# A linear attention kernel on one core: Q read in longer runs, norms and transposes moved, and another order in the last groups

## The chip, the cores and the metric

The kernel runs on one core of a Trainium2 chip. The time is the device time of one execution in microseconds (us). Each kernel was run several times, and a median is quoted with its range. The profile is of one of these executions; its span is about 1.8 us shorter than the time of that execution. A run is called slow when it lies more than 1.5% above the fastest of the same kernel. With one core there is no second die to compare with. Medians and ranges here are of all runs, slow ones too; ratios are of the fast runs alone.

The names of the engines in the profile: PE is TensorE, PEld its weight loads, DVE is VectorE, ACT is ScalarE, POOL is GpSimd, SP is SyncE.

## The reference

For each of 8 x 12 heads, with 512 rows of 64 numbers in Q, K and V:

```python
Q_feat = np.maximum(0, Q) + 1
K_feat = np.maximum(0, K) + 1
KV = np.einsum('bhkd,bhkv->bhdv', K_feat, V)
K_sum = np.sum(K_feat, axis=2)
numerator = np.einsum('bhqd,bhdv->bhqv', Q_feat, KV)
denominator = np.einsum('bhqd,bhd->bhq', Q_feat, K_sum)
return (numerator / (denominator[:, :, :, None] + 1e-10)).astype(np.float32)
```

All data are fp32 in HBM: 37.75 MB are read and 12.58 MB written.

## The kernel before

The 96 heads are worked in 12 groups of 8 heads. A group's work has these steps, each a function:

```python
def k_features(g):   # DVE: kf = max(K + 1, 1), two instructions
def v_blocks(g):     # V into a block layout: three copies on DVE, the fourth on ACT
def q_features(g):   # DVE: qf = max(Q + 1, 1), two instructions
def keys_values(g):  # PE: 32 matmuls into kva_ps, then four ACT copies into kva_diag
def transposes(g):   # PE: 16 transposes of qf into PSUM; ACT copies both halves to qt
def output(g):       # PE: 32 matmuls qt x kva_diag; DVE: 4 x (reciprocal, multiply) -> o_sb
```

K, V and Q are loaded for two groups at a time (the first and the last pair one group at a time), cast to bf16 on the way, from two buffers per tensor. A load is issued on POOL's queue as soon as its buffer is free. The instructions stand on each engine in the order of the program:

```python
for g in range(NG - 1):
    k_features(g)
    v_blocks(g)
    q_features(g)
    if g:
        transposes(g - 1)
    if g >= 2:
        output(g - 2)
    keys_values(g)
    if g % 2 and g // 2 + 2 < NG // 2:
        load_pair(g // 2 + 2)
    if g >= LAG:
        store(g - LAG)
last = NG - 1
k_features(last)
v_blocks(last)
transposes(last - 1)
output(last - 2)
q_features(last)
keys_values(last)
transposes(last)
output(last - 1)
output(last)
for g in range(last - LAG, NG):   # groups 10 and 11 in two halves each, from SP
    store(g)
```

In this text "the norms" are the reciprocal-multiply pairs of output, "K11" are the K features of group 11, "V10" is the copying of V of group 10 (with "lands", its transfer), and "group 10's matmuls" are the 32 of keys_values.

Of the kernel before, what the change touches and what calls it, by code (L numbers as in the profile page):

```python
# [9 lines left out]
BF16 = mybir.dt.bfloat16  # L10
# [9 lines left out]
def kernel(  # L20
# [15 lines left out]



    nc = tc.nc

    B, H, S, D = Q.shape
    P = 128
    C = 8
    C2 = 2 * C
    NPAIR = B * H * S // (P * C)
    NP = 4
    NG = NPAIR // NP
    D1 = D + 1
    W = 2 * D1

    def view(t, c):
        return t.flatten_outer_dims().rearrange("(n p c) d -> p n c d", p=P, c=c)

    q_dram = view(Q, C2)
    k_dram = view(K, C2)
    v_dram = view(V, C2)
    o_dram = view(out, C)
# [1 line left out]
    const = ctx.enter_context(tc.tile_pool(name="const", bufs=1))  # L59
    head_pool = ctx.enter_context(tc.tile_pool(name="head_pool", bufs=1))  # L60
    in_pool = ctx.enter_context(tc.tile_pool(name="in_pool", bufs=IN_BUFS))
    feat_pool = ctx.enter_context(tc.tile_pool(name="feat", bufs=2))
    mid_pool = ctx.enter_context(tc.tile_pool(name="mid", bufs=3))
    out_pool = ctx.enter_context(tc.tile_pool(name="out_pool", bufs=OUT_BUFS))
    recip_pool = ctx.enter_context(tc.tile_pool(name="recip", bufs=4))
    psum_kva = ctx.enter_context(tc.tile_pool(name="psum_kva", bufs=2, space=bass.MemoryType.PSUM))
# [1 line left out]
    psum_qt = ctx.enter_context(tc.tile_pool(name="psum_qt", bufs=2, space=bass.MemoryType.PSUM))  # L68

    identity = const.tile([P, P], BF16, name="identity")  # L70
    NV = 3
    v_all = const.tile([P, 9, 2, C2, D], BF16, name="v_all")
    v_blk = [v_all[:, 5 * i : 5 * i + 4] for i in range(2)]
    ones = const.tile([P, 4], BF16, name="ones")
    zero = const.tile([P, 1], FP32, name="zero")
    kva_diag = [const.tile([P, 4, 2, D1], BF16, name=f"kva_diag{i}") for i in range(NV)]

    drams = dict(k=k_dram, v=v_dram, q=q_dram)
    raw = {}
    kfs = {}  # L80
    qfs = {}
    qts = {}
    outs = {}

    def own(g):
        return slice(g % 2 * 2, g % 2 * 2 + 2)

    def load_first_k():
        k_raw = head_pool.tile([P, 2, C2, D], FP32, name="k_first")
        nc.sync.dma_start(out=k_raw, in_=k_dram[:, 0:2])  # L90
        raw["k", 0] = k_raw

    def load(s, groups, names="kvq"):
        ms = slice(groups[0] % 2 * 2, groups[-1] % 2 * 2 + 2)
        for x in names:
            if (x, "buf", s) not in raw:
                raw[x, "buf", s] = in_pool.tile([P, 4, C2, D], BF16, name=f"{x}_raw")
            t = raw[x, "buf", s]
            nc.gpsimd.dma_start(  # L99
                out=t[:, ms], in_=drams[x][:, 2 * groups[0] : 2 * groups[-1] + 2]  # L100
            )
            for g in groups:
                raw[x, g] = t[:, own(g)]

    def load_pair(s):
        if s < NG // 2 - 1:
            load(s, (2 * s, 2 * s + 1))
        else:
            load(s, (2 * s,))
            load(s, (2 * s + 1,))  # L110

    def store(g):
        o_sb = outs.pop(g)
        o_to = o_dram[:, g * NP : g * NP + NP]
        if g < NG - 2:
            nc.gpsimd.dma_start(out=o_to, in_=o_sb)  # L116
            return
        for h in range(2):
            nc.sync.dma_start(out=o_to[:, h:NP:2], in_=o_sb[:, h:NP:2])

    def feature(dst, src):
        nc.vector.tensor_scalar(  # L122
            out=dst, in0=src, scalar1=1.0, scalar2=1.0, op0=ALU.add, op1=ALU.max
        )

    def k_features(g):
        k_raw = raw.pop(("k", g))
        kf = feat_pool.tile([P, C2, 2, D], BF16, name="kf")
        for n in range(2):
            feature(kf[:, :, n], k_raw[:, n])  # L130
        kfs[g] = kf

    def v_blocks(g):
        v_raw = raw.pop(("v", g))
        for b in range(4):
            ps = slice(32 * b, 32 * b + 32)
            if b == 3:
                nc.scalar.copy(out=v_blk[g % 2][ps, b], in_=v_raw[ps])  # L138
            else:
                nc.vector.tensor_copy(out=v_blk[g % 2][ps, b], in_=v_raw[ps])  # L140

    def q_features(g):
        q_raw = raw.pop(("q", g))
        qf = feat_pool.tile([P, C2, 2, D], BF16, name="qf")
        for half in range(2):
            cs = slice(half * C, half * C + C)
            feature(qf[:, cs].rearrange("p c n d -> p n c d"), q_raw[:, :, cs])
        qfs[g] = qf

    def keys_values(g):  # L150
        kf = kfs.pop(g)
        sb = g % 2
        vb = v_all[:, 4 * sb : 4 * sb + 5]
        kva_ps = psum_kva.tile([P, 5, D], FP32, name="kva_ps")
        for c in range(C2):
            for n in range(2):
                nc.tensor.matmul(  # L157
                    kva_ps[64 * n : 64 * n + 64],
                    lhsT=kf[:, c, n, :],
                    rhs=vb[:, :, n, c, :],  # L160
                    start=(c == 0),
                    stop=(c == C2 - 1),
                )
        kva = kva_diag[g % NV]
        for n in range(2):
            ps = slice(64 * n, 64 * n + 64)
            nc.scalar.copy(out=kva[ps, :, n, 0:D], in_=kva_ps[ps, sb : sb + 4, :])  # L167
            nc.scalar.copy(out=kva[ps, :, n, D], in_=kva_ps[ps, 4 - 4 * sb, 0:4])  # L168

    def transposes(g):  # L170
        qf = qfs.pop(g)
        qt = mid_pool.tile([P, C, P, 2], BF16, name="qt")
        for half in range(2):
            qt_ps = psum_qt.tile([P, C, P], BF16, name="qt_ps")
            for c in range(C):
                nc.tensor.transpose(qt_ps[:, c, :], qf[:, half * C + c, :, :], identity)  # L176
            nc.scalar.copy(out=qt[:, :, :, half], in_=qt_ps)  # L177
        qts[g] = qt

    def output(g):  # L180
        kva = kva_diag[g % NV]
        qt = qts.pop(g)
        o_sb = out_pool.tile([P, NP, C, D], FP32, name="o_sb")
        for h in range(2):
            ops = [psum.tile([P, 2, BANK], FP32, tag="ps", name="o_ps") for _ in range(2)]
            for c in range(C):
                for j in range(2):
                    b = 2 * h + j
                    nc.tensor.matmul(  # L189
                        ops[c // 4][64 * j : 64 * j + 64, c // 2 % 2, (c % 2) * W : (c % 2) * W + W],  # L190
                        lhsT=qt[:, c, 32 * b : 32 * b + 32, :],
                        rhs=kva[:, b],
                        start=True,
                        stop=True,
                    )
            for i in range(2):
                cells = ops[i][:, :, 0 : 2 * W].rearrange("p b (c n x) -> p b c n x", n=2, x=D1)
                recip = recip_pool.tile([P, 2, 2, 2, 1], FP32, name="recip")
                nc.vector.reciprocal(out=recip, in_=cells[:, :, :, :, D:D1])  # L199
                nc.vector.tensor_tensor(  # L200
                    out=o_sb[:, h:NP:2, 4 * i : 4 * i + 4].rearrange(
                        "p n (b c) d -> p b c n d", b=2
                    ),
                    in0=cells[:, :, :, :, 0:D],
                    in1=recip.to_broadcast([P, 2, 2, 2, D]),
                    op=ALU.mult,
                )
        outs[g] = o_sb
# [9 lines left out]
    with tc.manual_schedule():  # L218
        nc.gpsimd.memset(zero, 0.0)
        load_first_k()  # L220
        load(0, (0,), "vq")
        load(0, (1,))
        nc.vector.memset(ones, 0.0)
        for b in range(4):
            nc.vector.memset(ones[32 * b : 32 * b + 32, b : b + 1], 1.0)  # L225
        clear(0, 3, 5)
        e = v_all[:, 4, :, :, 0:4].rearrange("p n c j -> p (n c) j")
        nc.vector.tensor_copy(out=e, in_=ones[:, None, :].to_broadcast([P, 2 * C2, 4]))
        make_identity(nc, identity)
        for t in kva_diag:  # L230
            nc.gpsimd.memset(t, 0.0)  # L231
        load_pair(1)
        clear(5, 7, 9)
        for g in range(NG - 1):
            k_features(g)
            v_blocks(g)
            q_features(g)
            if g:
                transposes(g - 1)
            if g >= 2:  # L240
                output(g - 2)
            keys_values(g)
            if g % 2 and g // 2 + 2 < NG // 2:
                load_pair(g // 2 + 2)
            if g >= LAG:
                store(g - LAG)
        last = NG - 1
        k_features(last)
        v_blocks(last)
        transposes(last - 1)  # L250
        output(last - 2)
        q_features(last)
        keys_values(last)
        transposes(last)
        output(last - 1)
        output(last)
        for g in range(last - LAG, NG):
            store(g)
# [30 lines left out]
```

## Time and profile before

| what | before |
|---|---|
| time, median of 4 runs | 127.41 us (127.02 to 128.06) |
| span of the profiled run | 125.8 us |
| DVE busy | 88.2 us (70%) |
| ACT busy | 68.0 us (54%) |
| PE busy | 65.2 us (52%) |
| mean rate of the HBM over the span | 400 GB/s |
| last DVE instruction ends | 120.36 us |
| last store lands | 124.87 us |

DVE is the busiest engine that computes, and yet it is idle for nearly a third of the span. The list of DVE's waits (who waited for whom: us in total, times, longest) says why:

```profile
DVE v_all L140 <- DMA v_raw<-in_V_dram: 10.6, 3, 5.3
DVE qf L122 <- DMA q_raw<-in_Q_dram: 6.5, 4, 2.9
...
DVE recip L199 <- PE o_ps L189: 4.8, 4, 1.7
```

It waits for loads, and only 4.8 us for PE. The prediction shows the other lines.

### The profile page before, as it was taken

The numbers are of one execution on the slowest core, as the hardware profiler recorded it, in microseconds if no ns is written. First come the engines' busy times: TensorE is split into PE (matmuls) and PEld (weight loads), VectorE is DVE, ScalarE is ACT, GpSimd is POOL, SyncE is SP. The second block draws the span as 40 slices with busy tenths as digits, with TensorE's granted clock in tenths as the row PEclk, the third lists the DMA queues.
The fourth block names the chain that finished last, engine by engine and source line by source line (L and its number), as shares of the span: only waits on it lengthen the run. The fifth ranks groups of instructions, "written<-read, shape, count | busy, mean of one in ns | idle before, by whom it ended". The sixth has DMA issues, their size and how long they took to land.

```text
span 125.8 us, 2337 instructions
## 1 busy us (share of the span) xinstructions
PE 65.2 (52%) x960; PEld 48.4 (39%) x960; DVE 88.2 (70%) x188; ACT 68.0 (54%) x87; POOL 27.8 (22%) x43
## 2 busy tenths in 40 slices
PE   0005939000059784796918476006978569694500
PEld 0003627000036564574806365004656447472300
DVE  4896280206199799999989990629959999758920
ACT  7832296006700889629892962750087971987000
POOL 6990213000002082023700260212221002020000
PEclk9999999755555999689999999955589976999955
DMA  3999999999999999999999999999999999999991
GB/s 76 341 211 209 210 213 211 210 212 211 212 211 212 211 214 212 210 212 214 253 414 287 209 210 212 213 369 380 209 210 210 211 287 418 418 417 410 403 391 72
DMA packets 13419, 32.13 MB, mean 255 GB/s; under 512 B 608, under 2 KB 608, under 8 KB 13408
## 3 DMA queue, kind: packets, MB, share of 16 engines
q0 software_dynamic: 12048, 28.84, 98.3%
q1 hardware_dynamic: 1360, 3.15, 6.8%
q8 instruction: 7, 0.11, 0.3%
q14 instruction: 4, 0.03, 0.1%
HBM read 37.75 MB, written 12.58 MB: 400 GB/s over the span
## 4 chain that ended last, share of the span: by engine, by line
DMA 40%; DVE 26%; PE 18%; POOL 6%; issue 6%; DVEq 0%; POOLq 0%
DMA q_raw<-in_Q_dram 40%; DVE o_sb L200 15%; PE kva_ps L157 11%; DVE v_all L140 4%; PE qt_ps L176 3%; DVE recip L199 3%; PE o_ps L189 3%; POOL v_raw L99 2%; DVE qf L122 2%; DVE kf L122 2%; POOL q_raw L99 1%; POOL kva_diag L231 1%; POOL k_raw L99 1%; POOL identity masks.py:199 0%; POOL identity masks.py:197 0%
## 5 line engine op out<-in xcount | busy, mean ns | idle before, releaser
L157 PE MATMUL kva_ps<-v_all,kf 128*64 128x320 bf16 x384 | 36.4, 356 | 13.1 <-DVE v_all L140 13.1
L189 PE MATMUL o_ps<-kva_diag,qt 128*64 128x130 bf16 x384 | 19.1, 234 | 40.9 <-DVE o_sb L200 40.4
L200 DVE TENSOR_TENSOR o_sb<-o_ps,recip 128x512 f32<-128x512 f32 x48 | 33.2, 692 | 1.6
L140 DVE COPY v_all<-v_raw 32x2048 bf16<-32x2048 bf16 x36 | 26.5, 736 | 10.9 <-DMA v_raw<-in_V_dram 10.6
L157 PEld LDWEIGHTS <-kf 128*64 128x64 bf16 x384 | 25.3, 133 | 20.9 <-DVE v_all L140 13.3
L189 PEld LDWEIGHTS <-qt 128*64 128x64 bf16 x384 | 12.7, 114 | 46.4 <-DVE o_sb L200 44.6
L138 ACT COPY v_all<-v_raw 32x2048 bf16<-32x2048 bf16 x12 | 22.7, 1894 | 13.3 <-DMA v_raw<-in_V_dram 13.1
L177 ACT COPY qt<-qt_ps 128x1024 bf16<-128x1024 bf16 x24 | 29.7, 1308 | 0.3
L167 ACT CAST kva_diag<-kva_ps 64x256 bf16<-64x256 f32 x24 | 8.9, 371 | 33.3 <-PE kva_ps L157 33.2
L122 DVE TENSOR_SCALAR qf<-q_raw 128x1024 bf16<-128x1024 bf16 x24 | 9.1, 423 | 6.6 <-DMA q_raw<-in_Q_dram 6.5
L99 POOL DMA_DIRECT2D k_raw<-in_K_dram x7 | 5.3, 754 | 38.1 <-DVE kf L122 37.3
L116 POOL DMA_DIRECT2D out_dram<-o_sb x10 | 8.4, 846 | 22.6 <-DVE o_sb L200 16.4
L176 PE MATMUL qt_ps<-identity,qf 128*128 128x128 bf16 x192 | 13.1, 222 | 0.0
L199 DVE RECIPROCAL recip<-o_ps 128x8 f32<-128x8 f32 x48 | 9.6, 199 | 4.9 <-PE o_ps L189 4.8
L122 DVE TENSOR_SCALAR kf<-k_raw 128x1024 bf16<-128x1024 bf16 x22 | 8.7, 437 | 6.0 <-DMA k_raw<-in_K_dram 6.0
L176 PEld LDWEIGHTS <-qf 128*128 128x128 bf16 x192 | 11.0, 99 | 3.3 <-issue 3.0
L99 POOL DMA_DIRECT2D v_raw<-in_V_dram x8 | 6.1, 764 | 18.8 <-ACT v_all L138 10.7
L99 POOL DMA_DIRECT2D q_raw<-in_Q_dram x8 | 5.9, 741 | 4.2 <-DMA q_raw<-in_Q_dram 4.2
L213 DVE MEMSET v_all<- 128x3072 f32 (+1 forms) x2 | 4.4, 2192 | 1.1 <-DVE ones L225 0.7
L168 ACT CAST kva_diag<-kva_ps 64x4 bf16<-64x4 f32 x24 | 4.0, 169 | 0.0
L214 ACT COPY v_all<-zero 128x2048 f32<-128x2048 f32 x2 | 3.7, 1894 | 0.0
L214 ACT ACT_TABLE_LOAD x1 | 1.3, 1283 | 0.7 <-PEq L273 0.7
(12 smaller groups left out, 4.6 us busy)
## 6 DMA issues: line engine op xcount, KB each, us to landing
out_dram<-o_sb POOLq DMA_DIRECT2D x10, 1024.0 KB, 20.2
k_raw<-in_K_dram POOLq DMA_DIRECT2D x4, 1024.0 KB, 18.0
v_raw<-in_V_dram POOLq DMA_DIRECT2D x4, 1024.0 KB, 20.9
q_raw<-in_Q_dram POOLq DMA_DIRECT2D x4, 1024.0 KB, 25.0
v_raw<-in_V_dram POOLq DMA_DIRECT2D x4, 512.0 KB, 17.3
q_raw<-in_Q_dram POOLq DMA_DIRECT2D x4, 512.0 KB, 17.1
out_dram<-o_sb SPq DMA_DIRECT2D x4, 512.0 KB, 5.1
k_raw<-in_K_dram POOLq DMA_DIRECT2D x3, 512.0 KB, 23.3
```

Of the source, the lines that this page charges most:

```text
L99: nc.gpsimd.dma_start(out=t[:, ms], in_=drams[x][:, 2 * groups[0] : 2 * groups[-1] + 2])
L116: nc.gpsimd.dma_start(out=o_to, in_=o_sb)
L122: nc.vector.tensor_scalar(out=dst, in0=src, scalar1=1.0, scalar2=1.0, op0=ALU.add, op1=ALU.max)
L138: nc.scalar.copy(out=v_blk[g % 2][ps, b], in_=v_raw[ps])
L140: nc.vector.tensor_copy(out=v_blk[g % 2][ps, b], in_=v_raw[ps])
L157: nc.tensor.matmul(kva_ps[64 * n : 64 * n + 64], lhsT=kf[:, c, n, :], rhs=vb[:, :, n, c, :], start=(c == 0), stop=(c == C2 - 1),)
L167: nc.scalar.copy(out=kva[ps, :, n, 0:D], in_=kva_ps[ps, sb : sb + 4, :])
L176: nc.tensor.transpose(qt_ps[:, c, :], qf[:, half * C + c, :, :], identity)
L177: nc.scalar.copy(out=qt[:, :, :, half], in_=qt_ps)
L189: nc.tensor.matmul(ops[c // 4][64 * j : 64 * j + 64, c // 2 % 2, (c % 2) * W : (c % 2) * W + W], lhsT=qt[:, c, 32 * b : 32 * b + 32, :], r ...
L199: nc.vector.reciprocal(out=recip, in_=cells[:, :, :, :, D:D1])
L200: nc.vector.tensor_tensor(out=o_sb[:, h:NP:2, 4 * i : 4 * i + 4].rearrange("p n (b c) d -> p b c n d", b=2), in0=cells[:, :, :, :, 0:D], i ...
```

## The change

The intent: fewer and longer reads for Q, DVE work (the norms of group g-2) moved into the time in which DVE waits for V, and a tail with shorter waits. In full that is:

- Q of groups 2 to 9 is loaded with 8 KB runs in HBM. One run now holds rows of both groups of a pair, so the output of one group needs the kva_diag of both (four of them in place of three). The copies of the transposes now read PSUM with a stride and write qt in order, where they read in order and wrote every second element.
- For even groups output(g-2) stands ahead of V's copies. For odd groups transposes stand on both sides of the output, and both groups' Q features are taken at once.
- In the last pair K and V are loaded in one transfer for both groups. Group 10's V copies stand behind output 8, its Q features and transposes ahead of K11 and V11, and DVE copies the second half of the transposes of groups 10 and 11 where ACT did both halves.

```diff
+    q_eights = view(Q, C4)
...
+    def load_q(s):
+        t = in_pool.tile([P, 4, C2, D], BF16, name="q_raw").rearrange(
+            "p (n r) (q c) d -> p n (r q c) d", n=2, c=C
+        )
+        nc.gpsimd.dma_start(out=t, in_=q_eights[:, 2 * s : 2 * s + 2])
...
     def load_pair(s):
-        if s < NG // 2 - 1:
-            load(s, (2 * s, 2 * s + 1))
-        else:
-            load(s, (2 * s,))
-            load(s, (2 * s + 1,))
+        pair = (2 * s, 2 * s + 1)
+        load("k", pair)
+        load("v", pair)
+        if eights(2 * s):
+            load_q(s)
+        else:
+            for g in pair:
+                load("q", (g,))
...
+            copy = nc.vector.tensor_copy if half and g >= NG - 2 else nc.scalar.copy
+            copy(out=qts[g][:, lo : lo + CC // 2], in_=qt_ps.rearrange("p c r q -> p c q r"))
...
+        for g in range(last):
+            if g and not eights(g - 1):
+                transposes(g - 1)
+            elif eights(g) and g % 2:
+                transposes(g - 1)
             k_features(g)
-            v_blocks(g)
-            q_features(g)
-            if g:
-                transposes(g - 1)
+            if g % 2:
+                v_blocks(g)
+            if not eights(g) and g < last - 1:
+                q_features(g)
             if g >= 2:
                 output(g - 2)
+            if g % 2 == 0:
+                v_blocks(g)
+            elif eights(g):
+                transposes(g)
+            if eights(g) and g % 2 == 0:
+                q_features(g)
+                q_features(g + 1)
             keys_values(g)
...
+        q_features(last - 1)
+        transposes(last - 1)
         k_features(last)
         v_blocks(last)
-        transposes(last - 1)
         output(last - 2)
+        keys_values(last)
         q_features(last)
-        keys_values(last)
         transposes(last)
```

eights(g) is true for groups 2 to 9. Cuts are marked with "..."; declarations of pools, and how Q, qt and the stores are addressed, are left out.

More of the change, by code (lines that the diff above doesn't have):

```diff
@@ L44 @@
     C2 = 2 * C
+    C4 = 4 * C
     NPAIR = B * H * S // (P * C)
@@ L61 @@
     in_pool = ctx.enter_context(tc.tile_pool(name="in_pool", bufs=IN_BUFS))
-    feat_pool = ctx.enter_context(tc.tile_pool(name="feat", bufs=2))
-    mid_pool = ctx.enter_context(tc.tile_pool(name="mid", bufs=3))
+    kf_pool = ctx.enter_context(tc.tile_pool(name="kf_pool", bufs=2))
+    qf_pool = ctx.enter_context(tc.tile_pool(name="qf_pool", bufs=3))
+    mid_pool = ctx.enter_context(tc.tile_pool(name="mid", bufs=2))
     out_pool = ctx.enter_context(tc.tile_pool(name="out_pool", bufs=OUT_BUFS))
@@ L70 @@
     identity = const.tile([P, P], BF16, name="identity")
-    NV = 3
+    NV = 4
     v_all = const.tile([P, 9, 2, C2, D], BF16, name="v_all")
@@ L79 @@
     raw = {}
+    bufs = {}
     kfs = {}
@@ L83, with eights @@
     outs = {}
+    def eights(g):
+        return 2 <= g < NG - 2
     def own(g):
-        return slice(g % 2 * 2, g % 2 * 2 + 2)
+        return slice(g % 2, 4, 2) if eights(g) else slice(g % 2 * 2, g % 2 * 2 + 2)
     def load_first_k():
@@ L91, in load_first_k, with load @@
         raw["k", 0] = k_raw
-    def load(s, groups, names="kvq"):
+    def load(x, groups):
+        s = groups[0] // 2
+        if groups[0] % 2 == 0 or (x, s) not in bufs:
+            bufs[x, s] = in_pool.tile([P, 4, C2, D], BF16, name=f"{x}_raw")
         ms = slice(groups[0] % 2 * 2, groups[-1] % 2 * 2 + 2)
-        for x in names:
-            if (x, "buf", s) not in raw:
-                raw[x, "buf", s] = in_pool.tile([P, 4, C2, D], BF16, name=f"{x}_raw")
-            t = raw[x, "buf", s]
-            nc.gpsimd.dma_start(
-                out=t[:, ms], in_=drams[x][:, 2 * groups[0] : 2 * groups[-1] + 2]
-            )
-            for g in groups:
-                raw[x, g] = t[:, own(g)]
-    def load_pair(s):
-        if s < NG // 2 - 1:
-            load(s, (2 * s, 2 * s + 1))
-        else:
-            load(s, (2 * s,))
-            load(s, (2 * s + 1,))
+        nc.gpsimd.dma_start(
+            out=bufs[x, s][:, ms], in_=drams[x][:, 2 * groups[0] : 2 * groups[-1] + 2]
+        )
+        for g in groups:
+            raw[x, g] = bufs[x, s][:, own(g)]
+    def load_q(s):
+        t = in_pool.tile([P, 4, C2, D], BF16, name="q_raw").rearrange(
+            "p (n r) (q c) d -> p n (r q c) d", n=2, c=C
+        )
+        nc.gpsimd.dma_start(out=t, in_=q_eights[:, 2 * s : 2 * s + 2])
+        rows = t.rearrange("p n (r c) d -> p n r c d", c=C)
+        for e in range(2):
+            raw["q", 2 * s + e] = rows[:, :, :, 4 * e : 4 * e + 4]
+    def load_pair(s):
+        pair = (2 * s, 2 * s + 1)
[3 more added lines that the diff above has]
+            load_q(s)
+        else:
+            for g in pair:
+                load("q", (g,))
     def store(g):
         o_sb = outs.pop(g)
-        o_to = o_dram[:, g * NP : g * NP + NP]
+        first = 2 * NP * (g // 2)
+        o_to = o_dram[:, first + g % 2 : first + 2 * NP : 2] if eights(g) else o_dram[
+            :, g * NP : g * NP + NP
+        ]
         if g < NG - 2:
@@ L127, in k_features @@
         k_raw = raw.pop(("k", g))
-        kf = feat_pool.tile([P, C2, 2, D], BF16, name="kf")
+        kf = kf_pool.tile([P, C2, 2, D], BF16, name="kf")
         for n in range(2):
@@ L143, in q_features @@
         q_raw = raw.pop(("q", g))
-        qf = feat_pool.tile([P, C2, 2, D], BF16, name="qf")
-        for half in range(2):
-            cs = slice(half * C, half * C + C)
-            feature(qf[:, cs].rearrange("p c n d -> p n c d"), q_raw[:, :, cs])
+        if not eights(g):
+            q_raw = q_raw.rearrange("p n (r c) d -> p n r c d", c=C)
+        R, CC = q_raw.shape[2:4]
+        qf = qf_pool.tile([P, R, CC, 2, D], BF16, name="qf")
+        for n in range(2):
+            feature(qf[:, :, :, n], q_raw[:, n])
         qfs[g] = qf
@@ L171, in transposes @@
         qf = qfs.pop(g)
-        qt = mid_pool.tile([P, C, P, 2], BF16, name="qt")
-        for half in range(2):
-            qt_ps = psum_qt.tile([P, C, P], BF16, name="qt_ps")
-            for c in range(C):
-                nc.tensor.transpose(qt_ps[:, c, :], qf[:, half * C + c, :, :], identity)
-            nc.scalar.copy(out=qt[:, :, :, half], in_=qt_ps)
-        qts[g] = qt
+        R, CC = qf.shape[1:3]
+        if R == 4 and g % 2:
+            qts[g] = qts[g - 1]
+        else:
+            qts[g] = mid_pool.tile([P, C, P, R], BF16, name=f"qt{R}")
+        first = g % 2 * CC if R == 4 else 0
+        for half in range(2):
+            qt_ps = psum_qt.tile([P, CC // 2, R, P], BF16, name="qt_ps")
+            for c in range(CC // 2):
+                for r in range(R):
+                    nc.tensor.transpose(
+                        qt_ps[:, c, r], qf[:, r, half * CC // 2 + c, :, :], identity
+                    )
+            lo = first + half * CC // 2
+            copy = nc.vector.tensor_copy if half and g >= NG - 2 else nc.scalar.copy
+            copy(out=qts[g][:, lo : lo + CC // 2], in_=qt_ps.rearrange("p c r q -> p c q r"))
     def output(g):
-        kva = kva_diag[g % NV]
         qt = qts.pop(g)
@@ L187, in output @@
                 for j in range(2):
-                    b = 2 * h + j
+                    if eights(g):
+                        b = 2 * (g % 2) + j
+                        kva = kva_diag[(g // 2 * 2 + h) % NV]
+                        q = slice(16 * (4 * h + b), 16 * (4 * h + b) + 16)
+                    else:
+                        b = 2 * h + j
+                        kva = kva_diag[g % NV]
+                        q = slice(32 * b, 32 * b + 32)
                     nc.tensor.matmul(
                         ops[c // 4][64 * j : 64 * j + 64, c // 2 % 2, (c % 2) * W : (c % 2) * W + W],
-                        lhsT=qt[:, c, 32 * b : 32 * b + 32, :],
+                        lhsT=qt[:, c, q, :],
                         rhs=kva[:, b],
@@ L220 @@
         load_first_k()
-        load(0, (0,), "vq")
-        load(0, (1,))
+        load("v", (0,))
+        load("q", (0,))
+        for x in "kvq":
+            load(x, (1,))
         nc.vector.memset(ones, 0.0)
@@ L233 @@
         clear(5, 7, 9)
-        for g in range(NG - 1):
+        last = NG - 1
+        for g in range(last):
[3 more added lines that the diff above has]
+                transposes(g - 1)
             k_features(g)
-            v_blocks(g)
-            q_features(g)
-            if g:
-                transposes(g - 1)
+            if g % 2:
+                v_blocks(g)
+            if not eights(g) and g < last - 1:
+                q_features(g)
             if g >= 2:
                 output(g - 2)
+            if g % 2 == 0:
[5 more added lines that the diff above has]
+                q_features(g + 1)
             keys_values(g)
@@ L246 @@
                 store(g - LAG)
-        last = NG - 1
+        q_features(last - 1)
+        transposes(last - 1)
         k_features(last)
         v_blocks(last)
-        transposes(last - 1)
         output(last - 2)
+        keys_values(last)
         q_features(last)
-        keys_values(last)
         transposes(last)
```

## The prediction

> **What bounds the kernel now.** I read the page's slices first, then a table of stretches, then the chain of waits, then the groups.
>
> ```profile
> DMA  3999999999999999999999999999999999999991
> GB/s 76 341 211 209 210 213 211 210 212 211 212 211 212 211 214 212 210 212 214 253 414 287 209 210 212 213 369 380 209 210 210 211 287 418 418 417 410 403 391 72
> HBM read 37.75 MB, written 12.58 MB: 400 GB/s over the span
> ```
>
> The DMA engines are busy from the second slice to the last but one. A load counts by what it writes (bf16, half of what it reads), so 212 GB/s of loads is 424 GB/s of HBM reads; stores run at about 418. One group's share of one tensor is 1.05 MB on the HBM side, and one such unit takes 1.05 MB / 0.42 = 2.5 us of the DMA, load or store. There are 48 units: 48 x 2.5 = 120 us of a 125.8 us span. The rest is about 2 us before the first packet and the end.
>
> ```profile
> 102.00:104.00 2.00, 1.91 (x22) 1.42 (x24) 1.93 (x7) 0.95 (x1) 0.00 (x0) 0.58 1.07 350
> 104.00:106.00 2.00, 2.00 (x20) 1.42 (x18) 1.97 (x5) 0.00 (x0) 0.75 (x1) 0.56 1.03 420
> 116.00:118.00 2.00, 0.94 (x20) 0.64 (x22) 1.90 (x7) 0.00 (x0) 0.00 (x0) 1.00 1.02 413
> 120.00:122.00 2.00, 0.00 (x0) 0.00 (x0) 0.36 (x1) 0.00 (x0) 0.00 (x0) 0.50 1.00 387
> 122.00:124.00 2.00, 0.00 (x0) 0.00 (x0) 0.00 (x0) 0.00 (x0) 0.00 (x0) 0.50 0.60 234
> ```
>
> Columns: stretch, length, busy us (count) of PE, PEld, DVE, ACT, POOL, then granted clock, DMA share, GB/s. The last loads land near 104 us; after that there are only stores, back to back until about 123. Compute (DVE) stops at 120.36 and the DMA still works off what was queued.
>
> ```profile
> 59.53 24.54 DMA q_raw<-in_Q_dram
> ...
> 87.24 4.27 PE kva_ps L157 x32
> ...
> 102.55 3.81 PE kva_ps L157 x32
> ...
> 109.99 2.17 PE kva_ps L157 x32
> ...
> 119.67 0.69 DVE o_sb L200
> ```
>
> This is the chain that ended last: start, length, what. It is a chain of compute from 84.07 (Q of groups 8 and 9 lands: 59.53 + 24.54) to 120.36. But the completion events of the stores in the trace come every 2.5 us (1.27 us for the half-size ones) right up to the last at 124.87, so the chain is not late: the DMA would end there even if compute ended sooner. How much sooner or later? An unloaded half-size store takes, from this trace, 1.07 us (issue to first packet, at the head) + 1.27 + 0.32 (last packet to completion) = 2.7 us. 124.87 - 2.7 = 122.2: compute has about 1.8 us of slack and no more. The same 32 matmuls take 2.2 us at full clock and 3.8 to 4.3 when the clock column says about 0.5. That matters below.
>
> ```profile
> L200 DVE TENSOR_TENSOR o_sb<-o_ps,recip 128x512 f32<-128x512 f32 x48 | 33.2, 692 | 1.6
> L140 DVE COPY v_all<-v_raw 32x2048 bf16<-32x2048 bf16 x36 | 26.5, 736 | 10.9 <-DMA v_raw<-in_V_dram 10.6
> L177 ACT COPY qt<-qt_ps 128x1024 bf16<-128x1024 bf16 x24 | 29.7, 1308 | 0.3
> L122 DVE TENSOR_SCALAR kf<-k_raw 128x1024 bf16<-128x1024 bf16 x22 | 8.7, 437 | 6.0 <-DMA k_raw<-in_K_dram 6.0
> ```
>
> DVE's bill per group: K features 0.7, V copies 3 x 0.736 = 2.2, Q features 0.76, an output of four reciprocal-multiply pairs 4 x 0.84 = 3.4 (each pair starts 0.84 after the last).
>
> [...] stores in 4 KB packets run at 418 to 420 GB/s, those in 2 KB packets near 413. [...] its halved stretches last 3.41 us or multiples, and windows with less than about half PE work were followed by one. [...] No such bf16 copy on DVE is in this trace; 512 fp32 elements from PSUM took 0.692, so I estimate 1.15 us for 1024 elements.
>
> **The change part by part.**
>
> Q in 8 KB runs. 8 groups, 8 x 128 x 2 = 2048 reads of 4 KB become 1024 of 8 KB. Over 16 engines that is 64 packets fewer each[...]
>
> Order in the middle. DVE takes the output of g-2 before it waits for V and Q of an even group, and both Q features at once. That moves 3.4 us of DVE work into its idle stretches (from 75.7 to 84.1 before) and frees Q's buffers sooner. But the DMA queue holds at least 7 us of issued work at each load's issue, from the issue times and the rate. So nothing in the middle is on the path: zero.
>
> One more clearing on POOL (0.5 us at about 7 us) lies under the 15 us of loads already queued: zero.
>
> The tail. Three things change. First, the last pair's loads become K10+11, V10+11, Q10, Q11 instead of K10, V10, Q10, K11, V11, Q11. Second, DVE does output 8 before V10. Third, DVE takes half of the transposes' copies of groups 10 and 11, and in DVE's order the copy for group 10 stands ahead of K11 and V11, waiting for PE. I walk it with the durations above:
> - Q of 8 and 9 lands at 83.9. Two stores, K10+11 and V10+11 follow, 6 units. The trace's completion of the sixth unit is 99.7 (before, it was K11); less 0.2 is 99.5. Before, V10 was there at 94.8.
> - Q 8 and 9 features, K9, V9, output 7: DVE done near 92. It waits for K10+11 (94.6), does output 8 to about 99.8, then V10 to 102.0.
> - PE's 32 matmuls for group 10 start at 102.0, after about 4 us with almost no PE work, so at half clock: 4.2 us, to 106.2. Transposes 1.2: 107.4. DVE, idle since 102.9, copies: 108.5.
> - K11 0.7, V11 2.3: 111.5. Output 9: 114.9. PE, again idle for 4 us, starts group 11's matmuls behind output 9's last ones at 113.8: cold to 118.0. Transposes to 119.2, DVE copy to 120.3 (idle since its Q11 features at 115.7).
> - Outputs 10 and 11: 6.9 us, 127.2.
>
> Compute would end at 127.2 instead of 120.4. Of these 6.8 us, 1.8 go into the slack and 5.0 reach the end: span 127.2 + 2.7 + 0.9 (last completion to end of span, as before) = 130.8; plus 1.75 between span and time (127.54 - 125.8) makes 132.6.
>
> **The rivals.**
> 1. The clock stays up. With group 11's matmuls at full clock (2.4) compute ends at 125.4 and the time is 130.8; with both groups' so, 123.4 and 128.8. For it: 3.4 us windows fall by chance. Against it: group 10's start comes after two windows with well under half PE work, and the like was followed by half clock every time.
> 2. The DMA stays the bound to the end. [...] For it: the DMA was saturated through the whole of before, and the author tuned the tail. Against it: DVE's work after V10 lands, without any wait, is 2.2 + 0.76 + 1.15 + 0.7 + 2.3 + 3.4 + 0.76 + 1.15 + 6.9 = 19.3 us, so 118.9, and two waits for PE of at least 2 us each exceed the slack.
> 3. The 8 KB runs are worth far more than I can see, for instance 5% of Q's 20 us: 1 us, and all landings move up by as much: about 126.6 where the DMA binds, 131.6 where compute does. [...]
>
> **Range and chances.** Both cold 132.6 (one half), one warm 130.8 (a quarter), both warm 128.8 (a twentieth), DMA-bound 127.3 or near (a fifth): mean 130.9. Below 127.3 there is little room, above 133 only if the DVE copy is dearer than estimated. Over 2% slower begins at 130.1: 0.58; within 2%: 0.39; over 2% faster (125.0) would need 2.5 us less DMA time: 0.03.
>
> **What would show it.** Right: DMA saturated and GB/s as before until 104, then a hole in the last slices; output 8 ahead of V10; DVE idle before the group 10 and 11 copies from PSUM, put down to PE; clock near 0.5 at 102 to 106; last DVE instruction after 123 and about 4 us from there to the end of the span. Wrong: stores back to back to the end, the load phase over much before 103.5, or DVE's copies not waiting.

## The result, and the profile after

The changed kernel takes 133.08 us (median of 4 runs, 131.94 to 134.26), against 127.41 before. The ratio is 1.041, with a 95% interval of 1.032 to 1.050. Ratios here are the mean time of one kernel's fast runs over that of the other's of the same rounds, so not quite the ratio of the medians. The profiled run has a span of 131.6 us.

These are lines of the changed kernel's page, the span in 40 slices (of 3.3 us):

```profile
PEclk9999997568569999599995999968999779769855
DMA  3999999999999999999999999999999999936484
GB/s 82 329 210 209 210 211 213 210 221 208 210 212 217 218 205 213 211 216 235 412 289 206 212 219 220 400 328 212 213 210 216 388 418 421 375 115 228 169 313 158
```

Up to slice 35 the DMA row is full, as it was before. Then it breaks: 115, 228, 169, 313 GB/s, where there had been some 400 to the end. In stretches of 2 us (length; busy us and count of PE, PEld, DVE, ACT, POOL; clock, DMA share, GB/s):

```profile
112.00:114.00 2.00, 0.38 (x8) 0.30 (x8) 1.90 (x5) 0.00 (x0) 0.00 (x0) 0.94 1.03 420
114.00:116.00 2.00, 1.71 (x22) 1.18 (x20) 1.93 (x5) 0.00 (x0) 0.00 (x0) 0.50 0.52 207
116.00:118.00 2.00, 2.00 (x24) 1.49 (x22) 0.76 (x3) 0.00 (x0) 0.75 (x1) 0.71 0.15 59
120.00:122.00 2.00, 0.42 (x8) 0.25 (x8) 1.93 (x5) 0.33 (x1) 0.00 (x0) 1.00 0.23 86
```

The DMA has run out of stores to do by 115 us, and from there it waits for compute. This is the end of the chain that ended last (start, length, what):

```profile
102.93 0.69 DVE v_all L164
103.67 3.95 PE kva_ps L183 x32
107.62 1.01 PE qt_ps L208 x16
108.73 0.32 DVE qt L213
...
114.46 0.64 PE o_ps L230 x7
115.11 3.25 PE kva_ps L183 x31
118.36 1.01 PE qt_ps L208 x16
119.47 0.32 DVE qt L213
...
126.72 0.69 DVE o_sb L241
```

It goes twice through the same loop: V's copies or norms on DVE, a group's 32 matmuls and 16 transposes on PE, and then a copy out of PSUM on DVE. In DVE's timeline (start, length, instruction, idle time before it and what ended it) the two copies stand with their waits, and the list of DVE's waits has the total:

```profile
108.73 1.23 DVE L213 COPY qt<-qt_ps 128x1024 bf16<-128x1024 bf16 x1 [4.32 <-PE qt_ps L208]
119.47 1.23 DVE L213 COPY qt<-qt_ps 128x1024 bf16<-128x1024 bf16 x1 [2.71 <-PE qt_ps L208]
```

```profile
DVE recip L240 <- PE o_ps L230: 17.8, 9, 5.1
DVE qt L213 <- PE qt_ps L208: 7.0, 2, 4.3
...
DVE v_all L164 <- DMA v_raw<-in_V_dram: 1.5, 1, 1.5
```

Two copies that did not stand on DVE before cost it 7.0 us of waiting for PE. The norms wait 17.8 us for PE where they waited 4.8, but all nine of these waits end before 98 us, in the middle and not in the tail. The intent for V was met: DVE waits 1.5 us for it where it waited 10.6. DVE's last instruction ends at 127.41 instead of 120.36, and the last store lands at 130.23 instead of 124.87.

### The profile page after: what moved, and what is told of

It reads as the page before. It is cut to its first block, busy times and chain, and to the rows that moved or that the text cites. A ratio compares the mean times of both kernels' runs of the same rounds, so it can differ in the third digit from the quotient of the medians.

```text
span 131.6 us, 2339 instructions
## 1 busy us (share of the span) xinstructions
PE 72.3 (55%) x960; PEld 54.6 (41%) x960; DVE 90.1 (68%) x190; ACT 59.6 (45%) x85; POOL 26.6 (20%) x42
## 2 busy tenths in 40 slices
DMA packets 12363, 32.13 MB, mean 244 GB/s; under 512 B 576, under 2 KB 576, under 8 KB 12352
## 4 chain that ended last, share of the span: by engine, by line
PE 37%; DVE 31%; ACT 17%; DMA 7%; issue 4%; POOL 1%; DVEq 0%; ACTq 0%; POOLq 0%
PE kva_ps L183 32%; DVE o_sb L241 16%; DVE v_all L164 11%; ACT v_all L162 7%; ACT qt L213 7%; DMA q_raw<-in_Q_dram 7%; PE qt_ps L208 3%; DVE recip L240 3%; ACT kva_diag L193 2%; PE o_ps L230 1%; POOL v_raw L108 1%; DVE kf L146 1%; DVE qt L213 0%; ACT kva_diag L194 0%; DVE qf L146 0%
## 5 line engine op out<-in xcount | busy, mean ns | idle before, releaser
L183 PE MATMUL kva_ps<-v_all,kf 128*64 128x320 bf16 x384 | 42.2, 395 | 35.1 <-DVE v_all L164 30.3
L183 PEld LDWEIGHTS <-kf 128*64 128x64 bf16 x384 | 30.1, 146 | 44.5 <-DVE v_all L164 31.1
L164 DVE COPY v_all<-v_raw 32x2048 bf16<-32x2048 bf16 x36 | 25.8, 717 | 1.8 <-DMA v_raw<-in_V_dram 1.5
L230 PEld LDWEIGHTS <-qt 128*64 128x64 bf16 x384 | 13.2, 113 | 24.1 <-DVE o_sb L241 18.7
L240 DVE RECIPROCAL recip<-o_ps 128x8 f32<-128x8 f32 x48 | 9.6, 200 | 17.8 <-PE o_ps L230 17.8
L213 ACT COPY qt<-qt_ps 128x1024 bf16<-128x1024 bf16 x22 | 21.3, 1014 | 0.3
L140 POOL DMA_DIRECT2D out_dram<-o_sb x10 | 7.8, 784 | 32.1 <-DVE o_sb L241 30.4
L208 PEld LDWEIGHTS <-qf 128*128 128x128 bf16 x192 | 11.3, 101 | 2.9 <-issue 2.6
L108 POOL DMA_DIRECT2D k_raw<-in_K_dram x6 | 4.7, 779 | 31.3 <-DVE kf L146 31.3
L108 POOL DMA_DIRECT2D v_raw<-in_V_dram x7 | 5.4, 765 | 26.6 <-ACT v_all L162 26.1
L213 DVE COPY qt<-qt_ps 128x1024 bf16<-128x1024 bf16 x2 | 2.5, 1225 | 7.0 <-PE qt_ps L208 7.0
L108 POOL DMA_DIRECT2D q_raw<-in_Q_dram x4 | 2.9, 720 | 0.0
```

Of the source, the lines that this page charges most:

```text
L108: nc.gpsimd.dma_start(out=bufs[x, s][:, ms], in_=drams[x][:, 2 * groups[0] : 2 * groups[-1] + 2])
L140: nc.gpsimd.dma_start(out=o_to, in_=o_sb)
L164: nc.vector.tensor_copy(out=v_blk[g % 2][ps, b], in_=v_raw[ps])
L183: nc.tensor.matmul(kva_ps[64 * n : 64 * n + 64], lhsT=kf[:, c, n, :], rhs=vb[:, :, n, c, :], start=(c == 0), stop=(c == C2 - 1),)
L208: nc.tensor.transpose(qt_ps[:, c, r], qf[:, r, half * CC // 2 + c, :, :], identity)
L213: copy(out=qts[g][:, lo : lo + CC // 2], in_=qt_ps.rearrange("p c r q -> p c q r"))
```

## The experiments

Twelve kernels were run. Each had a correct result. Those of one batch ran on one chip and share its runs of the kernel before (127.46 to 127.49 us median in the three batches). Diffs are against the changed kernel unless said otherwise.

**The tail put back (e1_oldtail).** Only the part after group 9, the last pair's loads and the ACT copies are as in the kernel before:

```diff
-            copy = nc.vector.tensor_copy if half and g >= NG - 2 else nc.scalar.copy
+            copy = nc.scalar.copy
...
+        if s == NG // 2 - 1:
+            for g in pair:
+                for x in "kvq":
+                    load(x, (g,))
+            return
...
-            if g % 2:
+            if g % 2 or g == last - 1:
                 v_blocks(g)
-            if not eights(g) and g < last - 1:
+            if not eights(g):
                 q_features(g)
...
-            if g % 2 == 0:
+            if g % 2 == 0 and g < last - 1:
                 v_blocks(g)
...
-        q_features(last - 1)
-        transposes(last - 1)
         k_features(last)
         v_blocks(last)
+        transposes(last - 1)
         output(last - 2)
+        q_features(last)
         keys_values(last)
-        q_features(last)
```

> The changed kernel with the earlier kernel's tail: loads of groups 10 and 11 one group at a time, V10 and Q10 ahead of output 8 on DVE, the transposes of group 10 behind K11 and V11, all transpose copies on ACT. The 8 KB runs and the new order of groups 0 to 9 stay. Theory A (the tail costs all of it): the last DVE instruction moves from 127.4 to about 120, the stores go back to back to the end, the time is 127.2 to 127.8. Theory B (the new order of the middle costs it, as compute there is late): compute still ends after 123, the time is 129.5 or more. Theory C (the 8 KB runs are slow): the loads end later than 104 and the time stays above 130.

Measured: 126.94 us (126.59 to 127.30), ratio 0.9955 (0.9912 to 0.9998). The page's rate row of this kernel:

```profile
GB/s 80 338 213 211 210 206 210 209 219 210 210 210 216 218 211 210 210 213 222 243 420 291 188 205 220 211 341 393 230 210 215 206 278 412 419 412 413 407 396 101
```

The stores are back to back again, though DVE's last instruction ends at 116.8, 3.6 us before the kernel before. So the whole loss was in the tail (theory A; the time is even a little below what I wrote for it), and compute that ends earlier than 120 is worth little or nothing.

**The new tail on the kernel before (e8_newtail).** The converse, as a diff against the kernel before:

```diff
+        load(s, (2 * s, 2 * s + 1), "kv")
...
-            load(s, (2 * s,))
-            load(s, (2 * s + 1,))
+            load(s, (2 * s,), "q")
+            load(s, (2 * s + 1,), "q")
...
-            nc.scalar.copy(out=qt[:, :, :, half], in_=qt_ps)
+            copy = nc.vector.tensor_copy if half and g >= NG - 2 else nc.scalar.copy
+            copy(out=qt[:, :, :, half], in_=qt_ps)
...
-            v_blocks(g)
-            q_features(g)
+            if g < NG - 2:
+                v_blocks(g)
+                q_features(g)
...
+            if g == NG - 2:
+                v_blocks(g)
             keys_values(g)
...
+        q_features(last - 1)
+        transposes(last - 1)
         k_features(last)
         v_blocks(last)
-        transposes(last - 1)
         output(last - 2)
+        keys_values(last)
         q_features(last)
-        keys_values(last)
```

> The kernel before with the changed kernel's tail only: K and V of the last pair in one load each, output 8 ahead of V10 on DVE, Q10's features, its transposes and their copy ahead of K11 and V11, DVE taking half of the copies of groups 10 and 11. Groups 0 to 9 and Q's 4 KB runs as before. If the tail costs it: walked from the trace of before, V10's copies end at 104.5, group 10's matmuls at 107 to 108.5, DVE ends at 127 to 128.6, time 132.5 to 134.5. If the changed middle is needed for the loss: 127.3 to 129.5.

Measured: 132.68 us (132.14 to 134.87), ratio 1.040 (1.034 to 1.046). The tail alone makes nearly the whole loss (5.3 of 5.7 us). Its copies wait as in the changed kernel; in DVE's timeline:

```profile
108.97 1.30 DVE L179 COPY qt<-qt_ps 128x1024 bf16<-128x1024 bf16 x1 [4.29 <-PE qt_ps L177]
...
119.71 1.29 DVE L179 COPY qt<-qt_ps 128x1024 bf16<-128x1024 bf16 x1 [2.68 <-PE qt_ps L177]
```

**Group 10's transposes moved down again (e4_order).**

```diff
         q_features(last - 1)
-        transposes(last - 1)
         k_features(last)
         v_blocks(last)
+        transposes(last - 1)
         output(last - 2)
```

> The changed kernel with group 10's transposes moved down again, behind K11's features and V11's copies; the DVE half of the copies, the load order and the rest stay. If the wait of DVE for PE in front of K11 is what costs: DVE does K11 and V11 from 104.4 to 107.2 in the time in which it stood idle, then copies at 108.7, output 9 from 109.9; group 11's matmuls start near 112; DVE ends near 124.7, time 130.2 to 130.8. If the copies on DVE are what costs, wherever they stand: 132.5 to 133.5.

Measured: 128.17 us (127.24 to 129.26), ratio 1.003 (0.997 to 1.009). DVE's timeline has K11 and V11 where the wait was, and PE's has group 11's matmuls:

```profile
103.94 2.07 DVE L164 COPY v_all<-v_raw 32x2048 bf16<-32x2048 bf16 x3
107.76 1.23 DVE L213 COPY qt<-qt_ps 128x1024 bf16<-128x1024 bf16 x1 [1.75 <-PE qt_ps L208]
```

```profile
110.97 2.34 PE L183 MATMUL kva_ps<-v_all,kf 128*64 128x320 bf16 x32
```

One line moved gives back 4.9 of 5.7 us (133.08 to 128.17). I had walked 2.3 to 2.9. In this trace DVE ends 5.1 us earlier than in the changed kernel's (122.35 against 127.41): the wait is 2.6 us shorter; with a shorter gap ahead of them, group 11's matmuls took 2.34 us instead of 3.46 (PE's granted clock was 1.00 from 110 to 114 here, and 0.50 from 114 to 116 and 0.71 from 116 to 118 there); and 1.1 us stood already in V10's copies, which began at 100.24 instead of 101.30 (that part differs from run to run, see e2_head). The copies on DVE as such, 1.23 us each, are cheap where nothing waits behind them.

**All transpose copies on ACT (e3_actcopy).**

```diff
-            copy = nc.vector.tensor_copy if half and g >= NG - 2 else nc.scalar.copy
+            copy = nc.scalar.copy
```

> The changed kernel with the last two groups' transpose copies all on ACT. DVE then has nothing that waits for PE between Q10's features and K11, so its 4.3 us wait and the 1.2 us copy go from the place ahead of K11; ACT's V11 copy comes 1 us later (112.5). Walk from the changed kernel's times: output 9 ends near 112.5, group 11's matmuls start near 112.5 instead of 114.9, DVE ends near 124.5 to 125, time 130.2 to 130.8. Rival: ACT with its 2 more copies takes over as the wait, and the time stays at 132.5 to 133.5.

Measured: 128.97 us (127.34 to 130.20), ratio 1.015 (1.007 to 1.022). Two of the four runs count as slow, and the profiled one is the fastest (127.34); 2.0 us of its gain stood already in V10's copies, which began at 99.27. More came back than expected again, and again group 11's matmuls were at full clock (1.00 from 110 to 114); PE's timeline:

```profile
110.44 2.36 PE L183 MATMUL kva_ps<-v_all,kf 128*64 128x320 bf16 x32 [1.22 <-ACT v_all L162]
```

The releaser is as I had it: ACT's V11 copy, behind its transpose copies, is the wait that took DVE's place. It is only 1.2 us long.

**Spare matmuls that keep PE busy (e6_busy).**

```diff
+    def keep_busy(kva_ps, count):
+        for _ in range(count):
+            nc.tensor.matmul(
+                kva_ps[0:64, 0:2, :], lhsT=identity[:, 0:64], rhs=identity,
+                start=True, stop=True,
+            )
...
+        if g == NG - 2:
+            keep_busy(kva_ps, 48)
...
+            if g == NG - 3 and h:
+                kva_bufs[NG - 1] = psum_kva.tile([P, 5, D], FP32, name="kva_ps")
+                keep_busy(kva_bufs[NG - 1], 60)
```

> The changed kernel with 108 spare matmuls on the identity (48 ahead of group 10's keys-values matmuls, 60 inside output 9), into PSUM that the next real matmul overwrites, so that PE isn't idle while it waits for V10 and for output 9's norms. Nothing else moves. If the halved clock is part of the path: group 10's 32 matmuls take 2.35 us instead of 3.95, group 11's 2.35 instead of 3.46; DVE ends 2.5 us earlier, time 130.2 to 131. If the slow matmuls lie beside other waits: time unchanged, 132.5 to 133.5.

Measured: 129.30 us (128.87 to 131.04), ratio 1.014 (1.009 to 1.018). PE's timeline:

```profile
98.38 2.84 PE L178 MATMUL kva_ps<-identity 128*64 128x128 bf16 x48
102.04 2.36 PE L194 MATMUL kva_ps<-v_all,kf 128*64 128x320 bf16 x32 [0.81 <-DVE v_all L164]
...
111.49 2.34 PE L194 MATMUL kva_ps<-v_all,kf 128*64 128x320 bf16 x32
```

Useless work in PE's gaps gained 3.8 us. Of the 4.5 us by which DVE ends earlier than in the changed kernel's trace (122.87 against 127.41), 1.6 and 1.1 are the two groups' matmuls (3.95 to 2.36, 3.46 to 2.34, at a granted clock of 1.00), and 1.6 stood already in V10's copies, which began at 99.67 instead of 101.30. That part is not from the spare matmuls but from the middle of the kernel, and differs from run to run (see below). So the halved clock is on the path, worth 2.7 us here.

**V of group 0 copied ahead of Q0's features (e2_head).**

```diff
-            if g % 2:
+            if g % 2 or g == 0:
                 v_blocks(g)
...
-            if g % 2 == 0:
+            if g % 2 == 0 and g:
                 v_blocks(g)
```

> The changed kernel with one thing moved: on DVE, V of group 0 is copied before Q0's features, which wait for a later transfer. In the changed kernel group 0's matmuls start at 13.55 us, and from there a chain of compute with 17.3 us per pair of groups runs to group 10's V copies at 101.3, which are 2.4 us behind the landing of V10. Theory B (that chain is on the path): group 0's matmuls start near 10.7, V10 is copied at its landing near 99, everything after it is 2 to 2.4 us earlier, time 130.6 to 131.2. Theory A (only the order within the tail counts, the middle has slack): time as in the changed kernel, 133.

Measured: 131.54 us (130.89 to 132.80), ratio 1.033 (1.026 to 1.040). The medians differ by 1.5 us from the changed kernel's, which lies between what theories B and A say; the ratios of the fast runs differ by 0.8%, about 1.1 us, and their intervals overlap. V10's copies started at 99.68 in this trace, and DVE ended at 125.77. But in four other traces with the changed kernel's middle and without this move they started at 98.86 (e5_loads), 99.27 (e3_actcopy), 99.67 (e6_busy) and 100.24 us (e4_order). So the gain can be the spread of the middle, and that the move itself brings it is not shown.

What the traces do show is that the middle was not slack: it is a chain of compute that runs behind its loads. In the changed kernel's DVE timeline, V8's copies stand at 83.98, though V8 landed at 78.94; they stand behind output 6, and PE's group 8 behind them:

```profile
83.98 2.37 DVE L164 COPY v_all<-v_raw 32x2048 bf16<-32x2048 bf16 x3
```

```profile
86.40 4.04 PE L183 MATMUL kva_ps<-v_all,kf 128*64 128x320 bf16 x32 [3.55 <-DVE v_all L164]
```

The even groups' matmuls start at 34.79, 52.07, 69.08, 86.40 and 103.67, so every 17.0 to 17.3 us. A pair's loads and stores take 8 units of 2.5 us, 20 us. The chain is faster than the DMA, so a late start is made up slowly: V6, V8 and V10 were copied 8.3, 5.0 and 2.4 us after they landed. How late it is at group 3 stays to the end: in the changed kernel's trace and those of e3_actcopy to e6_busy, V10's copies begin 56.8 to 57.4 us after group 3's matmuls. And that goes with how fast PE worked in groups 0 to 2: their matmuls took together 13.2 us in the changed kernel's trace, 12.9 in e4_order, 12.2 in e3_actcopy, 11.6 in e6_busy and 11.3 in e5_loads, and group 3's started at 43.95, 43.23, 42.48, 42.66 and 41.88. That this causes the spread of the runs (131.94 to 134.26) is likely; five traces do not show it.

**V ahead of the norms again for even groups (e7_norms).**

```diff
-            if g % 2:
-                v_blocks(g)
+            v_blocks(g)
...
-            if g % 2 == 0:
-                v_blocks(g)
-            elif eights(g):
+            if g % 2 and eights(g):
                 transposes(g)
```

> The changed kernel with V's copies of the even groups ahead of the norms of g-2 on DVE again, for all even groups; output still ahead of the keys-values matmuls on PE. If the norms' new place is what costs: 129.5 or less. By my walk the tail's waits for PE stay as they are and only the middle chain gets some tenths to 1.5 us shorter: 131.3 to 132.8.

Measured: 133.05 us (132.76 to 133.82), ratio 1.045 (1.039 to 1.051). No gain, a little outside what I had written (131.3 to 132.8). V10 was copied at 99.05, 2.3 us sooner, but output 8's norms then stood behind it, PE's group 10 behind those, and it started at 103.42, where the changed kernel has 103.67. So the norms' new place is not the cause.

**The last pair's loads one group at a time (e5_loads).**

```diff
+        if s == NG // 2 - 1:
+            for g in pair:
+                for x in "kvq":
+                    load(x, (g,))
+            return
```

> The changed kernel with the last pair's loads again one group at a time (K10, V10, Q10, K11, V11, Q11), nothing else. V10 lands near 94.8 instead of 98.9. My walk has DVE busy with output 8 until V10's copies in either case (101.3 in the changed kernel's trace, 99.3 to 100.2 in two other runs with the same middle), so at most some tenths come back: 132 to 133.3. Rival: the merged loads are what made V10 late, as the prediction's text has it (V10 at 99.5 in place of 94.8), and 1.5 us or more comes back: 131.5 or less.

Measured: 131.79 us (130.66 to 132.78), ratio 1.026 (1.021 to 1.032). The median lies between the two expectations. The runs fall into two pairs, 130.66 and 130.85, and 132.73 and 132.78, which count as slow; the fast pair is 1.9 us below the changed kernel's fast runs, which is what the rival had. The trace, of a fast run, says how much of that the loads explain. V10's copies began at 98.86, right behind output 8; with the merged loads V10 lands at about that time (98.86 in the changed kernel's trace), and its copies began at 99.05 at the earliest in the traces. The merged K of groups 10 and 11 lands near 94, and DVE waited for it 0.4 to 1.3 us in four traces (e2_head, e3_actcopy, e6_busy, e7_norms), where here K10's features began at 92.77 without a wait. So the merged loads cost some tenths when the middle is on time. Another 0.5 us lies at the very end: from the last landing to the end of the span pass 0.90 us here and 1.40 to 1.42 in the six traces with the changed kernel's loads (0.91 before and in e8_newtail, which merges K and V but keeps Q's 4 KB runs). Why, I could not see. The rest can be the spread of the middle.

**8 KB against 4 KB, with the tail put back (e9_q8, e10_q4).** The first is e1_oldtail's kernel once more. The second reads the same bytes into the same places in 4 KB runs, five rounds each:

```diff
-        nc.gpsimd.dma_start(out=t, in_=q_eights[:, 2 * s : 2 * s + 2])
+        for r in range(2):
+            rs = slice(16 * r, 16 * r + 16)
+            nc.gpsimd.dma_start(out=t[:, :, rs], in_=q_eights[:, 2 * s : 2 * s + 2, rs])
```

> The first experiment's kernel again (8 KB runs, new order of groups 0 to 9, earlier tail), here as the partner of the next. The DMA sets its end: 126.6 to 127.2, 0.3 to 0.5 us below before.

> As its partner, but Q of groups 2 to 9 is read in 4 KB runs into the same places: two loads per pair of groups, each taking every other 4 KB. If per-packet cost is what the 8 KB runs save[...]: 0.1 to 0.4 us above the partner, near 127.1. If the runs' length does nothing: the same within 0.1. If 8 KB is worth a lot and hidden elsewhere: 1 us or more above.

Measured: 127.30 us (126.71 to 128.33), ratio 1.000 (0.996 to 1.004), with 8 KB; 127.50 us (126.89 to 127.80), ratio 1.000 (0.997 to 1.004), with 4 KB. The 0.2 us between the medians lies in the range that I had written for a per-packet cost (0.1 to 0.4), but it is smaller than the spread, and the ratios, each uncertain by 0.4% or 0.5 us, do not show it. What the runs' length is worth is too small to see here. That the first kernel gave 0.9955 in one batch and 1.000 in another says how far such ratios can be trusted.

**The tail put back and V0 first (e11_combo), and whole stores at the end (e12_best).** The second has, in addition to the first, groups 10 and 11 stored as the others are:

```diff
-        if g < NG - 2:
-            nc.gpsimd.dma_start(out=o_to, in_=o_sb)
-            return
-        for h in range(2):
-            nc.sync.dma_start(out=o_to[:, h:NP:2], in_=o_sb[:, h:NP:2])
+        nc.gpsimd.dma_start(out=o_to, in_=o_sb)
```

> The partner kernel with V of group 0 copied ahead of Q0's features, which gave 1.5 us in the changed kernel. With the earlier tail the DMA sets the end, so: no difference from the partner, within 0.2 us.

> The combination of the last one with groups 10 and 11 stored like the others, one 1 MB store each from GpSimd in 4 KB packets, in place of four half stores from SyncE in 2 KB packets. In the first experiment compute ends at 116.8 with 8 us of stores still queued, so an early start of halves is worth nothing, and 2.1 MB at 418 in place of about 402 GB/s is 0.2 us less: 126.5 to 126.9, a little below the partner. If the end of a GpSimd store costs more than SyncE's: 0.2 to 0.5 us above it.

Measured: e11_combo 126.82 us (126.57 to 127.56), ratio 0.9958 (0.9924 to 0.9992): the lowest of its batch and 0.4% under the kernel before. Against its partner e9_q8 it is 0.5 us lower in the median, more than the 0.2 that I had allowed, but their ranges overlap. e12_best 128.56 us (127.96 to 128.89), ratio 1.008 (1.005 to 1.012): 1.7 us worse than e11_combo, much more than I had allowed for. Its last store lands at 124.52, 0.35 us later than e11_combo's (124.17), but its span ends 2.2 us after that, and e11_combo's 0.9. So most of it lies between the last landing and the end of the program, when the last stores are GpSimd's. What the program does there I could not see; this stays open.

## Why the prediction was right or wrong

**The bound and the slack: right.** The DMA set the end of the kernel before, with little slack behind it. e1_oldtail, with compute 3.6 us earlier, ended where the DMA does. The way from compute's end to the last landing, 2.7 us by the prediction, was 2.8 us in the changed kernel (127.41 to 130.23). The signs that it named came too: the hole in the last slices, the two waits of DVE for PE, half clock (0.50) from 104 to 106, and 4.2 us from DVE's end to the end of the span.

**Q's runs: not contradicted.** The reads did become fewer: the page has 13419 DMA packets before and 12363 in the changed kernel. What that saves was an estimate of mine that no trace shows; the medians of e9_q8 and e10_q4 differ by 0.2 us, which is within noise. The landing of Q of groups 8 and 9 decides nothing: 83.82 in the changed kernel and 84.07 before, but 84.48 in e1_oldtail, which has the 8 KB runs too. Nor is it shown that shorter packets are slower. The stretch from 116 to 118, read as the 2 KB packets' 413 GB/s, held mostly 4 KB packets; SyncE's 2 KB packets ran alone from 120 to 122, at 387, and in e12_best that stretch, with 4 KB packets only, has 389.

**"Nothing in the middle is on the path: zero": wrong.** The DMA queue had work enough there, as I said, but I did not ask whether compute kept up with it. The middle is a chain of about 17.2 us per pair that runs behind its loads: in the changed kernel's trace V10's copies began at 101.30, 2.4 us after V10 landed, where my walk had 99.8. In four other traces with this middle they began from 98.86 to 100.24, so how much it costs differs from run to run. I had also not noticed that Q0's features were put ahead of V0's copies on DVE (group 0's matmuls start at 13.55 us instead of 10.72); that this is why the chain is late is not shown, as e2_head's gain is within the spread. Nor is the new middle the cause of the loss: with the old one V10's copies began at 101.57 (e8_newtail).

**The walk through the tail: right in its mechanism; its end agrees by errors that cancel, which is luck.** In the profiled execution (133.44 us) it had V10's copies done at 102.0 (measured 103.6, the lateness just named), group 10's matmuls in 4.2 us (3.95), its transposes done at 107.4 (108.6), the DVE copy in 1.15, an estimate (1.23), behind an idle DVE (4.32 us), and output 9 until 114.9 (116.1). Then group 11's matmuls took 3.46 us, not 4.2, since the clock came back in the middle of them (0.50 from 113.77 to 117.18, then 1.00), and the end was 127.41 for 127.2. From the last landing to the end of the span it had 0.9 us (1.4). The walk said 132.6 us, the median is 133.08. The copy took 1.23 us where K's features of as many elements took 0.43. They read SBUF; the copy's source is in PSUM and strided as well, and no run separates the two.

**The merged loads: named among the causes, and of little weight.** The walk itself had DVE busy until V10's landing, so it never needed them; in e5_loads I can assign some tenths to the landings and 0.5 us to the end of the program.

**The rivals.** A tail at full clock did not come by chance (where the windows lie did differ: the halved one at group 10 began at 102.33 before and at 103.53 in the changed kernel), but it can be forced: e6_busy. Against it stood that a window of less than about half PE work was followed by half clock every time; the trace of before has one just below half (1.65 of 3.41 us from 61.37) that was not, and those ahead of group 10 are far lower (0.06 us in the changed kernel). In e6_busy the matmuls were 2.7 us shorter, against 3.6 to 3.8 from my pairs of 4.2 and 2.4. That the DMA stays the bound failed because the waits exceeded the slack, as argued against it. Long runs worth 1 us failed in e10_q4.

**Range and chances.** I shaded the walk's 132.6 down to 130.9 for rivals that did not come. The median of 133.08 lies at the upper edge of the range, 0.08 above 133.0. The walk deserved more trust than the thought that a tail with so many small choices must have been tuned to be good.

**What the walk did not see** is how the parts multiply. Moving the copy behind K11 and V11 removes 2.6 us of waiting (4.32 to 1.75), and the shorter gap then leaves PE at full clock: in the two clock windows of 3.41 us ahead of the halving in the changed kernel PE was busy 2.25 and 0.14 us, in those of e4_order at the same place 2.00 and 2.75 us, and there the clock stayed full. Any one of three repairs (e4_order, e3_actcopy, e6_busy) gives back 3.8 to 4.9 of the 5.7 us by the medians, and they can't add up: with all of the tail put back, in e1_oldtail, it is 6.1 us, and there the DMA sets the end.

## What to carry to other kernels

DVE's copy waited 4.3 us for PE, and K11 and V11 behind it, which were ready, waited with it; so ask of each instruction that is moved up what stood behind it that was ready. This kernel is bound by the DMA, but its tail is bound by compute as soon as the slack (1.8 us) is used up, and there a wait counts more than once when it lets TensorE's clock fall (2.6 us of wait brought 1.1 us of slower matmuls with it). When a large rewrite loses, put back its last part alone and put that part alone into the old kernel: two runs here found where all of it was.

## What else the traces show

- TensorE's clock: the halved stretches, apart from the last in each trace, lasted 17.07, 3.41, 10.24 and 3.41 us before and 3.41 or 6.83 us in the changed kernel. Counted over the 3.41 us windows of these two traces: at full clock, the window with the most PE work that was followed by half clock had 1.89 us (changed kernel, 28.43 to 31.85), and the one with the least that was not had 1.65 us (before, 61.37 to 64.79; the 1.67 us from 115.99 to 119.40 were followed by it). At half clock, 2.73 us of work (before, 85.27 to 88.68) were followed by another halved window; that one was busy throughout, and full clock came at 92.09. The least work that was followed by full clock was 3.00 us (before, 51.13 to 54.55).
- ACT's copy of a 128x1024 bf16 block out of PSUM took 1308 ns with the destination written at every second element, and 1014 ns with the source strided and the destination contiguous. The line of the kernel before is in the prediction; this is the changed one's:

```profile
L213 ACT COPY qt<-qt_ps 128x1024 bf16<-128x1024 bf16 x22 | 21.3, 1014 | 0.3
```

- A last store from GpSimd at the end of the program: from the last landing to the end of the span 2.2 us passed in the one trace in which GpSimd had issued the last stores (e12_best), and 0.9 to 1.4 in the thirteen in which SyncE had.
